# Narrow score blocks in a two-layer attention trunk: one float32 product, or three rounded ones

## The chip, the cores and the metric

The kernel runs on one core of one Trainium2 chip. The metric is the device time of one execution in microseconds (us). A core has five engines with queues of their own: PE (TensorE: it loads a stationary operand of up to 128 x 128, "PEld" in the profile, and streams the columns of a moving operand past it), DVE (VectorE), ACT (ScalarE), POOL (GpSimd) and SP, which issues most of the transfers. Each engine works through its queue in order, and waits on semaphores for the others. Products are written to PSUM, everything else lies in SBUF.

## The reference, cut to what matters

256 tokens of width 2048 go through two layers. Each layer normalises, projects with one wide matrix, runs 16 attention heads of width 128, multiplies by a gate and projects back. All is float32.

```
# layer 0: 10 heads A (one shared key and value head; every query keeps its 64 best keys)
#          6 heads B (dilated bands)
# layer 1: 8 heads C (stick-breaking), 8 heads D (softmax with forget gates)
logits = einsum('bqhd,bshd->bhqs', qb, k) * HEAD_DIM ** -0.5     # every kind of head, masked causally
```

The tokens are two blocks of 128. A causal head needs three blocks of scores of 128 x 128: the first queries with the first keys, and the second queries with both halves of the keys. The first of these three is the "first block" below (for the heads C, whose scores are kept the other way round, it is the second keys with the second queries).

## The kernel before, in words

**Precision.** A float32 product on PE appears as two records in the trace. To get near float32 from rounded operands (type float32r, one record), the kernel splits a float32 tile into a high part, which ACT rounds, and a low part, which DVE makes as the difference, and adds three products: high x high, high x low, low x high. All projections go this way: line 264 makes the high part of a half piece of weights, line 265 the low part, and lines 300, 301 and 303 are the three products, for two blocks of tokens, 512 columns wide at most.

**Order of work.** project() runs through the 36 column groups of the four weight matrices (ORDER0, four groups P, ORDER1, four groups Q). Weights arrive by SP's queue (line 241), and are split three halves ahead (AHEAD). The heads are Python generators, started when the projection of their group is done. tick() counts projection work; one tick is one step of six products of 512 columns, and at each tick the generators whose delay has run out emit their next piece. So the heads' pieces lie between projection products in PE's queue, at places fixed when the program is written, and in the queues of ACT and DVE likewise.

**A head's scores.** turn() (line 358) transposes the rows of queries and keys by four PE transposes into one PSUM tile of 512 columns. For the heads B, C and D qk_turned() then makes, from that tile, `hi` (ACT, line 367, the last 384 columns, rounded), `f` (ACT, line 368, the first 256 columns, copied as float32) and `lo` (DVE, line 369, 384 columns). Two ticks later the scores are made. In softmax_head() (heads A, B, D) line 401 is the first block, one float32 product from `f`; the other two blocks are one group of 256 columns by three(), lines 373, 374 and 375: high x high, high x low, low x high. stick_head() (heads C) does the same with line 682. heads_a() does two heads at once, with lines 576, 577 and 578 in the place of 367 to 369, and with the shared keys in `kA` (float32, line 507), `kAh` and `kAl`, made once by keys_a(). Afterwards DVE reads the scores (line 408, or 685), ACT takes the exponentials (line 410), PE turns them (line 358), and weigh_out() multiplies them with the values in float32 (lines 384 to 386).

The index scores of heads A (index()) make their parts from a turned tile of 512 columns whole, on lines 524 (ACT, high) and 525 (DVE, low). Lines 656 to 660 are the cumulative sums of the forget gates, float32 products of odd shapes: lines 656 to 658 have 128 stationary columns and 8 moving ones, 659 and 660 have 8 stationary ones and 256 or 128 moving ones.

Of the kernel before, what the change touches and what calls it, by code (L numbers as in the profile page):

```python
# [7 lines left out]
F32 = mybir.dt.float32  # L8
BF16 = mybir.dt.bfloat16
F32R = mybir.dt.float32r  # L10
AF = mybir.ActivationFunctionType
OP = mybir.AluOpType
PSUM = bass.MemoryType.PSUM

P = 128
# [144 lines left out]
def trunk(ctx, tc, x, xT, g1, w0, wo0, w1, wo1, bf, gf, consts, rope, out):  # L160
    nc = tc.nc
    cp = ctx.enter_context(tc.tile_pool(name="cp", bufs=1))
    wp = ctx.enter_context(tc.tile_pool(name="wp", bufs=3))
    hp = ctx.enter_context(tc.tile_pool(name="hp", bufs=2))
# [30 lines left out]
    rr = cp.tile([P, 2, NT], F32, name="rr")  # L195
    nr1 = cp.tile([P, NT], F32, name="nr1")
    vA = hp.tile([P, NT, P], F32, name="vA", tag="vt", bufs=1)
    kA = hp.tile([P, P], F32, name="kA", tag="kA", bufs=1)
    kAh = hp.tile([P, SEQ], F32R, name="kAh", tag="kAh", bufs=1)
    kAl = hp.tile([P, SEQ], F32R, name="kAl", tag="kAl", bufs=1)  # L200
    ikh = hp.tile([P, 2, SEQ], F32R, name="ikh", tag="ikh", bufs=1)
# [3 lines left out]
    nbA = score  # L205
# [68 lines left out]
    def start(g):  # L274
        n = next(g, None)
        if n is not None:
            side.append([g, n])
# [83 lines left out]
    def qk_turned(srcs):  # L361

        pt = turn(srcs)
        f = hp.tile([P, 256], F32, name="qkf", tag="qkf", bufs=1)
        hi = hp.tile([P, 384], F32R, name="qkh", tag="qkh", bufs=1)
        lo = hp.tile([P, 384], F32R, name="qkl", tag="qkl", bufs=1)
        nc.scalar.activation(hi, pt[:, P:512], AF.Copy)
        nc.scalar.activation(f, pt[:, 0:256], AF.Copy)
        nc.vector.tensor_tensor(lo, pt[:, P:512], hi.bitcast(F32), op=OP.subtract)
        return f, hi, lo  # L370

    def three(o, ah, al, bh, bl):
        nc.tensor.matmul(o, ah, bh, start=True, stop=False)
        nc.tensor.matmul(o, ah, bl, start=False, stop=False)  # L374
        nc.tensor.matmul(o, al, bh, start=False, stop=True)

    def qk_of(t):
        f, hi, lo = t
        return f[:, 0:P], f[:, P:256], hi[:, 256:384], lo[:, 256:384], hi[:, 0:256], lo[:, 0:256]

    def weigh_out(pT, vs, u, sc, kt):

# [13 lines left out]

    def softmax_head(qk, nb, vs, u, rs, kt):

        q0, k0, q1h, q1l, kh, kl = qk
        pS = pa.tile([P, 384], F32, name="s", tag="s", bufs=1)  # L400
        nc.tensor.matmul(pS[:, 0:P], q0, k0, start=True, stop=True)  # L401
        three(pS[:, P:384], q1h, q1l, kh, kl)
        sn = hp.tile([P, 384], F32, name="sn", tag="sn", bufs=2)
        nm = hp.tile([P, NT], F32, name="nm", tag="nm", bufs=2)
        pr = hp.tile([P, 384], F32, name="pr", tag="pr", bufs=2)
        l = hp.tile([P, NT], F32, name="l", tag="l", bufs=2)
        for th, s in BLK:
            nc.vector.tensor_tensor_reduce(sn[:, s], pS[:, s], nb[:, s], op0=OP.add, op1=OP.min, scale=1.0,  # L408
                                           scalar=3.0e38, accum_out=nm[:, th:th + 1])
            nc.scalar.activation(pr[:, s], sn[:, s], AF.Exp, scale=-1.0, bias=nm[:, th:th + 1],  # L410
                                 accum_out=l[:, th:th + 1])
        yield 3
        pt = turn([pr[:, 0:P], pr[:, P:SEQ], pr[:, SEQ:384]])
        pT = hp.tile([P, 384], F32, name="pT", tag="pT", bufs=2)
        nc.scalar.activation(pT, pt[:, 0:384], AF.Copy)  # L415
        sc = hp.tile([P, NT], F32, name="sc", tag="sc", bufs=2)
        nc.vector.reciprocal(sc, l)
        nc.vector.tensor_tensor(sc, sc, rs, op=OP.mult)
        yield 2
        yield from weigh_out([pT[:, i * P:(i + 1) * P] for i in range(3)], vs, u, sc, kt)  # L420
# [75 lines left out]
    def keys_a(ps):  # L496
        kr = hp.tile([P, 512], F32, name="kr", tag="qk")
        for th in range(NT):
            rotate(kr[:, th * P:(th + 1) * P], ps[th][:, 0:P], rt[:, th, P:2 * P], rt[:, th, 3 * P:4 * P], 1, P)
            o = 256 + th * P  # L500
            rotate(kr[:, o:o + DI], ps[th][:, 256:320], rt[:, th, 512:576], rt[:, th, 576:640], 1, DI)
            nc.gpsimd.tensor_copy(kr[:, o + DI:o + P], kr[:, o:o + DI])
            nc.scalar.activation(vA[:, th, :], ps[th][:, P:2 * P], AF.Copy, scale=r0[:, th:th + 1])
            nc.vector.tensor_scalar(iw[:, th, :], ps[th][:, 320:336], r0[:, th:th + 1], None, op0=OP.mult)
        yield 4
        pt = turn([kr[:, i * P:(i + 1) * P] for i in range(4)])
        nc.scalar.activation(kA, pt[:, 0:P], AF.Copy)
        nc.scalar.activation(kAh, pt[:, 0:256], AF.Copy)
        nc.vector.tensor_tensor(kAl, pt[:, 0:256], kAh.bitcast(F32), op=OP.subtract)
        for j in range(2):  # L510
            d = slice(j * DI, (j + 1) * DI)
            nc.scalar.activation(ikh[d, j], pt[d, 256:512], AF.Copy)
            nc.vector.tensor_tensor(ikl[d, j], pt[d, 256:512], ikh[d, j].bitcast(F32), op=OP.subtract)
# [47 lines left out]
    def heads_a(ps, h):  # L561
        qk = hp.tile([P, 512], F32, name="qk", tag="qk")
        u = hp.tile([P, 2, NT, P], F32, name="u2", tag="u2", bufs=1)
        for th in range(NT):
            rotate(qk[:, th * 256:(th + 1) * 256], ps[th][:, 0:256], rt[:, th, 0:P], rt[:, th, 256:384], 2, P)
            tg = hp.tile([P, 256], F32, name="tg", tag="tg")
            nc.scalar.activation(tg, ps[th][:, 256:512], AF.Tanh, scale=hr0[:, th:th + 1])
            nc.vector.scalar_tensor_tensor(u[:, :, th, :], tg.rearrange("p (a b) -> p a b", a=2), 1.0,
                                           ps[th][:, 256:512].rearrange("p (a b) -> p a b", a=2),
                                           op0=OP.add, op1=OP.mult)  # L570
        yield 4
        pt = turn([qk[:, 0:P], qk[:, P:256], qk[:, 256:384], qk[:, 384:512]])
        f = hp.tile([P, 256], F32, name="qqf", tag="qkf", bufs=1)
        hi = hp.tile([P, 256], F32R, name="qqh", tag="qkh", bufs=1)
        lo = hp.tile([P, 256], F32R, name="qql", tag="qkl", bufs=1)
        nc.scalar.activation(hi, pt[:, 256:512], AF.Copy)
        nc.scalar.activation(f, pt[:, 0:256], AF.Copy)
        nc.vector.tensor_tensor(lo, pt[:, 256:512], hi.bitcast(F32), op=OP.subtract)
        yield 2
        js = [slice(j * P, (j + 1) * P) for j in range(2)]  # L580
        hs = [softmax_head((f[:, js[j]], kA, hi[:, js[j]], lo[:, js[j]], kAh, kAl), nbA, [vA[:, 0], vA[:, 1]],
                           u[:, j].rearrange("p a b -> p (a b)"), hr0, YPOS[f"A{h + j}"]) for j in range(2)]
        start(delay(hs[1], 2))
        yield from hs[0]

    def delay(g, n):
        yield n
        yield from g
# [88 lines left out]

    def stick_head(qk, v, u, kt):

        k1, q1, k0h, k0l, qh, ql = qk  # L680
        pZ = pa.tile([P, 384], F32, name="s", tag="s", bufs=1)
        nc.tensor.matmul(pZ[:, 0:P], k1, q1, start=True, stop=True)
        three(pZ[:, P:384], k0h, k0l, qh, ql)
        z = hp.tile([P, 384], F32, name="z", tag="sn")
        nc.vector.tensor_tensor(z, pZ, smask, op=OP.add)
        sp = hp.tile([P, 384], F32, name="sp", tag="pr")
        nc.scalar.activation(sp, z, AF.Abs)
        nc.scalar.activation(sp, sp, AF.Exp, scale=-1.0)
        nc.scalar.activation(sp, sp, AF.Ln, bias=1.0)
        nc.vector.scalar_tensor_tensor(sp, z, 0.0, sp, op0=OP.max, op1=OP.add)  # L690
        hi, lo = sph[:, P:512], spl[:, P:512]
        nc.scalar.activation(hi, sp, AF.Copy)
        nc.vector.tensor_tensor(lo, sp, hi.bitcast(F32), op=OP.subtract)
        yield 5
        pW = pa.tile([P, 384], F32, name="s", tag="s", bufs=1)
        nc.tensor.matmul(pW, tris[0], hi, start=True, stop=False)
        nc.tensor.matmul(pW, tris[0], lo, start=False, stop=False)
        nc.tensor.matmul(pW[:, 0:256], tris[1], sph[:, 0:256], start=False, stop=False)
        nc.tensor.matmul(pW[:, 0:256], tris[1], spl[:, 0:256], start=False, stop=True)
        w = hp.tile([P, 384], F32, name="wT", tag="pT")  # L700
        nc.vector.tensor_tensor(w, pW, z, op=OP.add)
        nc.scalar.activation(w, w, AF.Exp)
        yield 3
        yield from weigh_out([w[:, 256:384], w[:, P:256], w[:, 0:P]], [v[:, 0], v[:, 1]], u, r1, kt)
# [158 lines left out]
```

## Time and profile before

| what | value |
|---|---|
| median of the three runs | 934.88 us (934.54 to 936.18) |
| the profiled execution | 935.72 us |
| its span, first to last instruction | 933.9 us |
| mean granted TensorE clock | 0.996 |
| busy: PE, PEld | 921.2 us, 772.4 us |
| busy: DVE, ACT, POOL | 592.0 us, 474.8 us, 43.8 us |
| moved from and to HBM | 165.89 MB read, 2.11 MB written, 180 GB/s |

Times are from the hardware profiler, of one execution. PE is TensorE's product stream and PEld its weight loads, which run beside the products; ends of products are modelled, so the distance from one product to the next, as the chain of waits has it, says more than a record's own length. "<-" in a row reads "made from"; "x2" merges two records. In the chain of waits each row is a piece of the chain that ended last: its start, its length and what it was. A bracket in a timeline holds the time for which the engine stood idle before the instruction, and what ended it. Tile names are the program's: `qkh`, `qkl` and `qkf` are `hi`, `lo` and `f` of a head, `qqh`, `qql` and `qqf` those of a pair of heads A, `s` is the scores, `pj` a projection, `tp` a turned tile.

### The profile page before, as it was taken

The numbers are of one execution on the slowest core, as the hardware profiler recorded it, in microseconds if no ns is written. First come the engines' busy times: TensorE is split into PE (matmuls) and PEld (weight loads), VectorE is DVE, ScalarE is ACT, GpSimd is POOL, SyncE is SP. The second block draws the span as 40 slices with busy tenths as digits, with TensorE's granted clock in tenths as the row PEclk, the third lists the DMA queues.
The fourth block names the chain that finished last, engine by engine and source line by source line (L and its number), as shares of the span: only waits on it lengthen the run. The fifth ranks groups of instructions, "written<-read, shape, count | busy, mean of one in ns | idle before, by whom it ended". The sixth has DMA issues, their size and how long they took to land.

```text
span 933.9 us, 12009 instructions
## 1 busy us (share of the span) xinstructions
PE 921.2 (99%) x4537; PEld 772.4 (83%) x4537; DVE 592.0 (63%) x982; ACT 474.8 (51%) x805; POOL 43.8 (5%) x63
## 2 busy tenths in 40 slices
PE   9999999999999999999999999999999999999996
PEld 6978888888888888888898888888888888888876
DVE  7657777756556556555566666666766666665553
ACT  7654454544545545544456555555555444554441
POOL 0002100000000000000000000000000000001110
PEclk9999999999999999999999999999999999999998
DMA  9854445544455445555356444444655555455542
GB/s 346 342 180 175 144 172 181 175 169 139 150 180 180 163 156 178 180 184 189 126 171 245 159 157 165 160 175 180 231 186 186 172 172 174 175 180 180 182 179 91
DMA packets 27754, 168.77 MB, mean 181 GB/s; under 512 B 3224, under 2 KB 4784, under 8 KB 9520
## 3 DMA queue, kind: packets, MB, share of 16 engines
q1 hardware_dynamic: 26208, 165.24, 50.0%
q0 software_dynamic: 768, 2.12, 0.8%
q8 instruction: 35, 0.57, 0.2%
q10 hardware_dynamic: 720, 0.66, 0.2%
q14 instruction: 23, 0.19, 0.1%
HBM read 165.89 MB, written 2.11 MB: 180 GB/s over the span
## 4 chain that ended last, share of the span: by engine, by line
PE 92%; DMA 3%; issue 2%; ACT 1%; DVE 1%; SPq 0%; DVEq 0%; POOLq 0%; POOL 0%; ACTq 0%
PE pj L300 28%; PE pj L303 27%; PE pj L301 27%; PE tp L358 3%; DMA xs<-in_x_dram 1%; PE o L386 1%; PE o L385 1%; PE o L384 1%; DMA xst<-in_xT_dram 1%; DMA raw<-in_w_in_dram 1%; ACT sq L424 1%; DMA w0yh<-in_w_in_dram 1%; PE s L401 1%; ACT whi L264 0%; PE s L374 0%
## 5 line engine op out<-in xcount | busy, mean ns | idle before, releaser
L265 DVE TENSOR_TENSOR wlo<-raw,whi 128x1024 fp32r<-128x1024 f32 (+3 forms) x300 | 355.3, 1199 | 193.0 <-ACT whi L264 192.1
L300 PE MATMUL pj<-whi,xh 128*128 128x512 f32 (+3 forms) x992 | 387.3, 392 | 0.9 <-ACT whi L264 0.7
L301 PE MATMUL pj<-whi,xl 128*128 128x512 f32 (+3 forms) x992 | 377.0, 382 | 0.0
L264 ACT ACTIVATE whi<-raw 128x1024 fp32r<-128x1024 f32 (+3 forms) x300 | 302.0, 1025 | 133.3 <-PE pj L301 130.0
L303 PE MATMUL pj<-wlo,xh 128*128 128x512 f32 (+3 forms) x992 | 298.1, 382 | 0.1
L303 PEld LDWEIGHTS pj<-wlo,xh 128*128 128x128 f32 x992 | 183.5, 188 | 37.5 <-DVE wlo L265 0.9
L300 PEld LDWEIGHTS pj<-whi,xh 128*128 128x128 f32 x992 | 187.0, 188 | 33.1 <-ACT whi L264 2.5
L301 PEld LDWEIGHTS pj<-whi,xl 128*128 128x128 f32 x992 | 187.1, 189 | 30.4
L300 PE MATMUL pj<-whi,yh 128*128 128x512 f32 (+1 forms) x248 | 96.2, 388 | 0.0
L301 PE MATMUL pj<-whi,yl 128*128 128x512 f32 (+1 forms) x248 | 94.9, 383 | 0.0
L303 PE MATMUL pj<-wlo,yh 128*128 128x512 f32 (+1 forms) x248 | 76.7, 383 | 0.0
L303 PEld LDWEIGHTS pj<-wlo,yh 128*128 128x128 f32 x248 | 46.6, 188 | 9.2
L300 PEld LDWEIGHTS pj<-whi,yh 128*128 128x128 f32 x248 | 46.7, 188 | 8.6
L301 PEld LDWEIGHTS pj<-whi,yl 128*128 128x128 f32 x248 | 46.7, 188 | 8.5
L410 ACT ACTIVATE pr<-sn,nm 128x128 f32<-128x128 f32 (+1 forms) x48 | 21.5, 448 | 47.8 <-DVE nm L408 47.8
L394 ACT ACTIVATE yh<-tp 128x256 fp32r<-128x256 f32 x32 | 12.3, 385 | 57.5 <-PE tp L358 57.4
L395 DVE TENSOR_TENSOR yl<-tp,yh 128x256 fp32r<-128x256 f32 x32 | 13.6, 425 | 25.9 <-ACT yh L394 25.0
L424 ACT ACTIVATE sq<-xs 128x512 f32<-128x512 f32 x23 | 14.3, 623 | 30.3 <-DVE xs L594 27.7
L637 DVE RECIPROCAL e<-e 128x256 f32<-128x256 f32 x16 | 28.1, 1754 | 0.5
L353 POOL TENSOR_TENSOR qk<-rot,rot 128x256 f32<-128x256 f32 x22 | 16.0, 738 | 239.8 <-DVE rot L352 239.8
L415 ACT ACTIVATE pT<-tp 128x384 f32<-128x384 f32 x24 | 11.7, 485 | 20.9 <-PE tp L358 20.9
L623 ACT ACTIVATE qk<-pj,rr 128x128 f32<-128x128 f32 x32 | 10.0, 364 | 21.3 <-PE pj L303 21.3
(203 smaller groups left out, 703.8 us busy)
## 6 DMA issues: line engine op xcount, KB each, us to landing
raw<-in_w_in_dram SPq DMA_DIRECT2D x108, 1024.0 KB, 4.8
raw<-in_w_out_dram SPq DMA_DIRECT2D x32, 1024.0 KB, 4.8
raw<-in_w_in_dram SPq DMA_DIRECT2D x4, 672.0 KB, 9.4
raw<-in_w_in_dram SPq DMA_DIRECT2D x4, 528.0 KB, 3.5
w0yl<-in_w_in_dram SPq DMA_DIRECT2D x4, 512.0 KB, 8.2
xs<-in_x_dram SPq DMA_DIRECT2D x2, 1024.0 KB, 11.3
raw<-in_w_in_dram SPq DMA_DIRECT2D x4, 512.0 KB, 3.9
xst<-in_xT_dram SPq DMA_DIRECT2D x5, 256.0 KB, 7.0
```

What stands on the lines that cost most here:

```text
L264: nc.scalar.activation(hi, rw, AF.Copy)
L265: nc.vector.tensor_tensor(lo, rw, hi.bitcast(F32), op=OP.subtract)
L300: nc.tensor.matmul(o, a, wh, start=(kt == 0), stop=False)
L301: nc.tensor.matmul(o, b, wh, start=False, stop=False)
L303: nc.tensor.matmul(o, a, wl, start=False, stop=(kt == KT - 1))
L353: nc.gpsimd.tensor_tensor(dst, t1[:, 0:n], t2[:, 0:n], op=OP.add)
L358: nc.tensor.transpose(pt[:, i * P:(i + 1) * P], s, ident)
L394: nc.scalar.activation(yh[:, kt, :], pt[:, 0:SEQ], AF.Copy)
L395: nc.vector.tensor_tensor(yl[:, kt, :], pt[:, 0:SEQ], yh[:, kt, :].bitcast(F32), op=OP.subtract)
L410: nc.scalar.activation(pr[:, s], sn[:, s], AF.Exp, scale=-1.0, bias=nm[:, th:th + 1], accum_out=l[:, th:th + 1])
L424: nc.scalar.activation(j, xs[:, th, c * 512:(c + 1) * 512], AF.Square, accum_out=ss[:, i, th, c:c + 1])
L637: nc.vector.reciprocal(e, e)
```

## The change

qk_turned() and heads_a() no longer make the float32 copy `f`. `hi` and `lo` cover all 512 columns of the turned tile. A new function scores() makes a head's first block as three rounded products of 128 columns in the order of three(), ahead of the group of 256 columns, which is as it was; softmax_head() and stick_head() call it. The float32 copy `kA` of the first keys goes, and the heads A use the first 128 columns of `kAh` and `kAl`. Nothing else changes.

```diff
@@ -195,7 +195,6 @@
     rr = cp.tile([P, 2, NT], F32, name="rr")
     nr1 = cp.tile([P, NT], F32, name="nr1")
     vA = hp.tile([P, NT, P], F32, name="vA", tag="vt", bufs=1)
-    kA = hp.tile([P, P], F32, name="kA", tag="kA", bufs=1)
     kAh = hp.tile([P, SEQ], F32R, name="kAh", tag="kAh", bufs=1)
     kAl = hp.tile([P, SEQ], F32R, name="kAl", tag="kAl", bufs=1)
     ikh = hp.tile([P, 2, SEQ], F32R, name="ikh", tag="ikh", bufs=1)
@@ -361,13 +360,11 @@
     def qk_turned(srcs):
 
         pt = turn(srcs)
-        f = hp.tile([P, 256], F32, name="qkf", tag="qkf", bufs=1)
-        hi = hp.tile([P, 384], F32R, name="qkh", tag="qkh", bufs=1)
-        lo = hp.tile([P, 384], F32R, name="qkl", tag="qkl", bufs=1)
-        nc.scalar.activation(hi, pt[:, P:512], AF.Copy)
-        nc.scalar.activation(f, pt[:, 0:256], AF.Copy)
-        nc.vector.tensor_tensor(lo, pt[:, P:512], hi.bitcast(F32), op=OP.subtract)
-        return f, hi, lo
+        hi = hp.tile([P, 512], F32R, name="qkh", tag="qkh", bufs=1)
+        lo = hp.tile([P, 512], F32R, name="qkl", tag="qkl", bufs=1)
+        nc.scalar.activation(hi, pt, AF.Copy)
+        nc.vector.tensor_tensor(lo, pt, hi.bitcast(F32), op=OP.subtract)
+        return hi, lo
 
     def three(o, ah, al, bh, bl):
         nc.tensor.matmul(o, ah, bh, start=True, stop=False)
@@ -375,8 +372,15 @@
         nc.tensor.matmul(o, al, bh, start=False, stop=True)
 
     def qk_of(t):
-        f, hi, lo = t
-        return f[:, 0:P], f[:, P:256], hi[:, 256:384], lo[:, 256:384], hi[:, 0:256], lo[:, 0:256]
+
+        hi, lo = t
+        return hi[:, 0:P], lo[:, 0:P], hi[:, 384:512], lo[:, 384:512], hi[:, P:384], lo[:, P:384]
+
+    def scores(o, qk):
+
+        ah, al, bh, bl, mh, ml = qk
+        three(o[:, 0:P], ah, al, mh[:, 0:P], ml[:, 0:P])
+        three(o[:, P:384], bh, bl, mh, ml)
 
     def weigh_out(pT, vs, u, sc, kt):
 
@@ -396,10 +400,8 @@
 
     def softmax_head(qk, nb, vs, u, rs, kt):
 
-        q0, k0, q1h, q1l, kh, kl = qk
         pS = pa.tile([P, 384], F32, name="s", tag="s", bufs=1)
-        nc.tensor.matmul(pS[:, 0:P], q0, k0, start=True, stop=True)
-        three(pS[:, P:384], q1h, q1l, kh, kl)
+        scores(pS, qk)
         sn = hp.tile([P, 384], F32, name="sn", tag="sn", bufs=2)
         nm = hp.tile([P, NT], F32, name="nm", tag="nm", bufs=2)
         pr = hp.tile([P, 384], F32, name="pr", tag="pr", bufs=2)
@@ -504,7 +506,6 @@
             nc.vector.tensor_scalar(iw[:, th, :], ps[th][:, 320:336], r0[:, th:th + 1], None, op0=OP.mult)
         yield 4
         pt = turn([kr[:, i * P:(i + 1) * P] for i in range(4)])
-        nc.scalar.activation(kA, pt[:, 0:P], AF.Copy)
         nc.scalar.activation(kAh, pt[:, 0:256], AF.Copy)
         nc.vector.tensor_tensor(kAl, pt[:, 0:256], kAh.bitcast(F32), op=OP.subtract)
         for j in range(2):
@@ -570,15 +571,14 @@
                                            op0=OP.add, op1=OP.mult)
         yield 4
         pt = turn([qk[:, 0:P], qk[:, P:256], qk[:, 256:384], qk[:, 384:512]])
-        f = hp.tile([P, 256], F32, name="qqf", tag="qkf", bufs=1)
-        hi = hp.tile([P, 256], F32R, name="qqh", tag="qkh", bufs=1)
-        lo = hp.tile([P, 256], F32R, name="qql", tag="qkl", bufs=1)
-        nc.scalar.activation(hi, pt[:, 256:512], AF.Copy)
-        nc.scalar.activation(f, pt[:, 0:256], AF.Copy)
-        nc.vector.tensor_tensor(lo, pt[:, 256:512], hi.bitcast(F32), op=OP.subtract)
+        hi = hp.tile([P, 512], F32R, name="qqh", tag="qkh", bufs=1)
+        lo = hp.tile([P, 512], F32R, name="qql", tag="qkl", bufs=1)
+        nc.scalar.activation(hi, pt, AF.Copy)
+        nc.vector.tensor_tensor(lo, pt, hi.bitcast(F32), op=OP.subtract)
         yield 2
         js = [slice(j * P, (j + 1) * P) for j in range(2)]
-        hs = [softmax_head((f[:, js[j]], kA, hi[:, js[j]], lo[:, js[j]], kAh, kAl), nbA, [vA[:, 0], vA[:, 1]],
+        j1 = [slice(256 + j * P, 256 + (j + 1) * P) for j in range(2)]
+        hs = [softmax_head((hi[:, js[j]], lo[:, js[j]], hi[:, j1[j]], lo[:, j1[j]], kAh, kAl), nbA, [vA[:, 0], vA[:, 1]],
                            u[:, j].rearrange("p a b -> p (a b)"), hr0, YPOS[f"A{h + j}"]) for j in range(2)]
         start(delay(hs[1], 2))
         yield from hs[0]
@@ -677,10 +677,8 @@
 
     def stick_head(qk, v, u, kt):
 
-        k1, q1, k0h, k0l, qh, ql = qk
         pZ = pa.tile([P, 384], F32, name="s", tag="s", bufs=1)
-        nc.tensor.matmul(pZ[:, 0:P], k1, q1, start=True, stop=True)
-        three(pZ[:, P:384], k0h, k0l, qh, ql)
+        scores(pZ, qk)
         z = hp.tile([P, 384], F32, name="z", tag="sn")
         nc.vector.tensor_tensor(z, pZ, smask, op=OP.add)
         sp = hp.tile([P, 384], F32, name="sp", tag="pr")
```

## Rows read from the trace of the kernel before

**Rows 1.** The page of the kernel before: span, busiest engine, chain that ended last.
```profile
span 933.9 us, 12009 instructions
...
PE 921.2 (99%) x4537; PEld 772.4 (83%) x4537; DVE 592.0 (63%) x982; ACT 474.8 (51%) x805; POOL 43.8 (5%) x63
...
PE pj L300 28%; PE pj L303 27%; PE pj L301 27%; PE tp L358 3%; DMA xs<-in_x_dram 1%; PE o L386 1%; PE o L385 1%; PE o L384 1%; DMA xst<-in_xT_dram 1%; DMA raw<-in_w_in_dram 1%; ACT sq L424 1%; DMA w0yh<-in_w_in_dram 1%; PE s L401 1%; ACT whi L264 0%; PE s L374 0%
```

**Rows 2.** Chain of waits on PE, 840 to 842.2 us: start us, us, what.
```profile
841.04 0.22 PE s L401 x2
841.26 0.12 PE s L373
...
841.62 0.23 PE pj L300
```

**Rows 3.** Costliest groups by line and shape: busy us, mean ns, then idle before.
```profile
L369 DVE TENSOR_TENSOR qkl<-tp,qkh 128x384 fp32r<-128x384 f32 x22 | 12.1, 551 | 2.5 <-ACT qkf L368 2.5
...
L367 ACT ACTIVATE qkh<-tp 128x384 fp32r<-128x384 f32 x22 | 10.8, 492 | 15.7 <-PE tp L358 15.7
...
L368 ACT ACTIVATE qkf<-tp 128x256 f32<-128x256 f32 x22 | 8.4, 381 | 0.0
...
L401 PE MATMUL s<-qkf 128*128 128x128 f32 x28 | 5.3, 272 | 0.0
...
L525 DVE TENSOR_TENSOR il<-tp,ih 128x512 fp32r<-128x512 f32 x4 | 2.7, 684 | 1.1 <-ACT ih L524 1.1
...
L524 ACT ACTIVATE ih<-tp 128x512 fp32r<-128x512 f32 x4 | 2.4, 599 | 4.8 <-PE tp L358 4.8
```

**Rows 4.** Chain of waits, 469.9 to 473 us and 486 to 490 us.
```profile
469.85 0.33 PE tp L358 x3
...
488.31 0.22 PE s L657 x2
...
489.28 0.22 PE s L660 x2
```

**Rows 5.** Timeline of head C0 at 473 us: start us, us, instruction, [idle].
```profile
472.80 0.31 PEld L682 LDWEIGHTS s<-qkf 128*128 128x128 f32 x2
472.84 0.55 DVE L369 TENSOR_TENSOR qkl<-tp,qkh 128x384 fp32r<-128x384 f32 x1
...
473.44 0.19 PEld L374 LDWEIGHTS s<-qkl,qkh 128*128 128x128 f32 x1 [0.22 <-DVE qkl L369]
...
473.55 0.19 PEld L375 LDWEIGHTS s<-qkh,qkl 128*128 128x128 f32 x1
```

**Rows 6.** Timeline, heads C2 (524 us) and D7 (840 us): start, us, instruction.
```profile
524.53 0.55 DVE L369 TENSOR_TENSOR qkl<-tp,qkh 128x384 fp32r<-128x384 f32 x1
...
525.16 0.38 PE L682 MATMUL s<-qkf 128*128 128x128 f32 x2
...
840.27 0.55 DVE L369 TENSOR_TENSOR qkl<-tp,qkh 128x384 fp32r<-128x384 f32 x1
...
840.88 0.38 PE L401 MATMUL s<-qkf 128*128 128x128 f32 x2
```

**Rows 7.** Timeline of a pair of heads A at 231 us.
```profile
231.14 0.42 DVE L578 TENSOR_TENSOR qql<-tp,qqh 128x256 fp32r<-128x256 f32 x1
...
232.73 0.38 PE L401 MATMUL s<-kA,qqf 128*128 128x128 f32 x2
```

**Rows 8.** Chain of waits, 40 to 60 us, and timeline of PE there.
```profile
44.51 0.30 DVE qkl L369
...
44.92 0.38 PE L401 MATMUL s<-qkf 128*128 128x128 f32 x2
...
51.70 0.33 PE L358 MATMUL tp<-cons,pr 128*128 128x128 f32 x1 [1.96 <-ACT pr L410]
```

**Rows 9.** Waits of PE's weight loads over the span: us, times, longest.
```profile
PEld s L374 <- DVE qkl L369: 0.2, 1, 0.2
```

**Rows 10.** Busy us by stretch: PE, PEld, DVE, ACT, POOL, then granted clock.
```profile
50.00:55.00 5.00, 3.13 (x11) 2.65 (x12) 3.27 (x9) 2.86 (x9) 0.00 (x0) 0.70 0.60 208
```

## The prediction

> **What bounds the kernel now.** I read the page first. PE is busy for 921.2 of 933.9 us, and the chain that ended last runs for 82% of the span through the projection products of lines 300, 301 and 303 [rows 1]. DVE and ACT are busy for 592.0 and 474.8 us. So a nanosecond added to PE's stream is a nanosecond of the end, nearly everywhere, and work taken from ACT is worth nothing unless PE waits for it. A busy PE is not PE at its peak, so I read next what one product really takes: in the chain of waits a projection product of 512 columns takes 0.23 us, a rounded product of 256 columns 0.12, and the float32 product of a head's first block 0.22, in two records of 0.11 each [rows 2]. The reader is to see there that the first block, of 128 columns, costs as much as a projection product of 512.
>
> Third, the groups by line give the durations on ACT and DVE, and the number of records: 28 on line 401 for the 14 heads of kinds B and D, so two to a product [rows 3]. Last, the timelines around the scores, to see what PE's next weight load would wait for [rows 5 to 8]. Over the whole span a score waits for its low part once, for 0.2 us [rows 9]. How near the other heads are to such a wait is the second question here.
>
> **What the change does, part by part.**
>
> *Products.* There are 32 heads (6 B, 10 A, 8 C, 8 D). Each loses one float32 product, two records, 0.22 us in the chain [rows 2], and gets three rounded products of 128 columns. The kernel before has no rounded product as narrow as that, so its cost has to be bounded. From below: if only the moving columns counted, the line through 256 columns at 0.12 and 512 at 0.23 [rows 2] gives 0.12 - 128 x 0.11/256 = 0.065 us. From above: each as long as the whole float32 product, 0.22. Between them stand the rows of short products. Line 657 multiplies 128 loaded columns with 8 moving ones, and its two records take 0.22, as much as the 128 moving columns of a score; line 660 has 8 loaded columns and 128 moving ones and takes 0.22 as well [rows 4]. So a weight load of 128 columns takes 0.11 by itself, however little moves behind it, and a float32 record of 128 moving columns takes 0.11 too. The transposes, one record of 128 by 128, also take 0.11 each [rows 4]. That rounded operands don't load faster is seen at head C0: after a wait that left nothing to hide behind, the load of line 375 starts 0.11 us behind that of line 374, both rounded [rows 5]. That row is the nearest to the new product, so I take 0.11: three cost 0.33, 0.11 more than now. For 32 heads that is 3.5 us; with 31 of them (B0 stands below) 3.4 us. The ends are -0.8 us (32 x (3 x 0.065 - 0.22)) and +14.1 us (32 x 0.44).
>
> One rule speaks for a smaller term: the Trainium skill, page "TensorE: Matmul & The Clock Gate", section "Back-to-back issue gap", gives about 81 ns per load and product of 128 columns in a sustained stream. By it three would take 0.24 us and the term would be an estimated 0.7 us instead of 3.5; the trace disagrees, at 0.11 us each in the transposes [rows 4].
>
> *ACT.* A head of kind B, C or D now rounds 384 columns in 492 ns and copies 256 in 381; it will round 512 in one instruction, for which line 524 gives 599 [rows 3]. That is 274 ns less, 22 times: 6.0 us of ACT time. The A pairs and the copy of line 507 shrink likewise. It is worth nothing: in all the heads whose low part is late (next part), DVE starts it right behind other work of its own, long after ACT is done.
>
> *DVE, and the wait that moves.* The low part grows from 384 to 512 columns, 551 to 684 ns by line 525 [rows 3], so it lands 0.13 us later. And it is wanted sooner: today PE runs the two float32 records and line 373 before the first product that reads the low part; in the new order it is the second of the three narrow products. Its load can start when the first product starts to stream, which is where the first float32 record starts now. For head C2 that is 525.16 us, and the low part would be there at 524.53 + 0.684 = 525.21, and 0.05 later for PE (the lag at C0: 472.84 + 0.55 against the load at 473.44 [rows 5]): a wait of 0.10 us. For D7 it is 840.27 + 0.684 + 0.05 = 841.00 against 840.88, a wait of 0.12 [rows 6]. All 14 heads from C2 to D7 look like one of these two: 14 x 0.11 = 1.6 us. At C0 the wait exists already: the low part would be seen at 472.84 + 0.684 + 0.05 = 473.57, then come four loads of 0.11 (the second narrow product's, the third's, line 373's, then line 374's at 473.90) where line 374's is at 473.44 now [rows 5]; 0.46 later, of which 0.11 is counted above, so 0.35 us. The A pairs have room: 0.42 becomes 0.684 from 231.14 on, and PE comes at 232.73 [rows 7]. So have B1 to B5 and C1, whose low parts end well before PE comes.
>
> What queues behind the longer DVE instruction is the next low part of the weights, which is used several microseconds later; the bound for that delay is nothing as long as PE doesn't wait for line 265.
>
> *B0.* PE would lose 0.11 + 0.32 us there (44.51 + 0.684 + 0.05 against 44.92), but it stands idle for 1.96 us at 51.70, and the chain of that stretch runs through DVE, with this very low part in it [rows 8]. So PE's loss is covered, and DVE's 0.13 us counts. The granted clock falls to 0.70 in the 5 us around that idle time [rows 10]; if the idle time moves or shrinks, that is worth up to 0.3 x 5 = 1.5 us either way, which I keep for the range.
>
> No transfer and no issue on SP or POOL moves. The buffers that go or grow are on-chip and their sum stays within a kilobyte; I give that nothing.
>
> **Sum:** 3.4 + 1.6 + 0.35 + 0.13 = 5.5 us, 0.6%. The profiled execution took 935.72 us with a span of 933.9 [rows 1]; the median of the runs shown is 934.88, 0.84 below it. On the median the forecast is 940.4 us.
>
> **The rivals.**
>
> *The waits don't come.* If DVE gets to the low part 0.13 us sooner (ACT is freer ahead of it), only the products and B0 count: 3.5 us, 938.4. Against it: at the 14 heads DVE's queue is full in front of it. Chance 0.15.
>
> *Narrow rounded products run no faster than float32.* Nothing in the trace shows rounded operands under 256 columns, and the kernel might lose their speed there. At 0.22 each the products cost 14.1 us, and the waits vanish beneath them: 949. For it there is only the absence of such rows; against it, that 256 columns cost hardly more than half of 512 [rows 2]. Chance 0.10.
>
> *The moving columns set the pace, not the loads (not slower).* If PE can hide the loads of three products in a row, each takes 0.065: -0.8 us, plus the waits' 2.0 and B0's 0.13 give 1.3 us, 936.2, no change that can be measured. It decides where a load of 128 columns takes under 0.075 us, since then three cost no more than the 0.22 of now. Against it: line 657 and the loads at C0, both 0.11. The Trainium skill ("FP8 and Floating Point Precision", "TensorE Precision Notes") counts four passes for a float32 product; against three that would save a quarter of 0.22, an estimated 1.8 us, were it the passes that are paid. Chance 0.07.
>
> *Anything else*, such as the clock around 52 us: 0.03.
>
> **How the numbers follow.** The forecast has a chance of 0.65, its own range 939.0 to 941.9. A difference under 0.2% (1.9 us) can't be told from none. Slower is the sum of the forecast and the first two rivals, 0.90; same is 0.08, the third rival and a third of the rest; faster 0.02. The range goes down to 937.5 (the first rival, less 0.9 for half of the clock's stake) and up to 943.5 (the forecast with the waits doubled, 1.6, and the clock's 1.5): it leaves out the other two rivals and the rest, 0.20.
>
> **What would show it.** In the chain of waits the three narrow products take 0.33 us where the float32 pair took 0.22; if they show 0.2 or 0.66, the second or third rival holds. Among the waits of PE's weight loads, the low part of the score appears some 14 times with about 0.1 us each and once with 0.6 at C0. ACT's busy time falls by 6 us or more and DVE's rises by about 4 without either changing the end. A gain in time, or narrow loads closer than 0.11 us with no wait, would prove me wrong.

## The result, and the profile after

The changed kernel took 940.44 us (median of 4 runs, 939.13 to 942.2), the kernel before 934.71 beside it (4 runs). The ratio is 1.0061, 95% interval 1.0043 to 1.0079: slower by 5.7 us. The profiled execution took 942.2 us.

The page of the changed kernel, lines that answer to [rows 1]: span, busy time of the engines, the chain by line, and ACT's high part, which is one instruction of 512 columns now.

```profile
span 940.4 us, 12008 instructions
...
PE 928.0 (99%) x4569; PEld 777.8 (83%) x4569; DVE 596.1 (63%) x982; ACT 471.7 (50%) x777; POOL 43.8 (5%) x63
...
PE pj L299 29%; PE pj L300 29%; PE pj L302 29%; PE tp L357 3%; PE s L371 1%; PE s L372 1%; PE s L370 1%; PE o L390 1%; PE o L389 1%; PE o L388 1%; PE tp L606 0%; DMA w0yh<-in_w_in_dram 0%; PE s L535 0%; PE s L534 0%; PE s L536 0%
...
L365 ACT ACTIVATE qkh<-tp 128x512 fp32r<-128x512 f32 x22 | 13.2, 600 | 15.7 <-PE tp L357 15.7
```

PE is busy for 6.8 us more and the span is 6.5 us longer. ACT has lost 3.1 us net and DVE has gained 4.1, without showing in the chain; the scores take more of it than before (1% on each of lines 370 to 372, where [rows 1] has 1% on line 401 and less on line 374).

Chain of waits on PE, in the stretch of a pair of heads A, the place of [rows 7]. Start us, us, what:

```profile
234.10 0.06 PE s L370
234.16 0.11 PE s L371
234.27 0.11 PE s L372
234.38 0.17 PE s L370
234.55 0.12 PE s L371
234.67 0.12 PE s L372
234.79 0.23 PE pj L299
```

These are the six products of one head. Together they take 0.69 us where the five records of [rows 2] took 0.22 + 3 x 0.12 = 0.58. The first of them seems cheap, 0.06: its load lay beneath the 512 columns before it, and only its own 128 columns are seen. So the three narrow rows add up to 0.28, not to the 0.33 that the prediction named as its sign; the other 0.05 stands in the row behind them. The loads of the second, the third and the first wide product come one per 0.11, and the last of these is paid by the wide product, which takes 0.17 rather than 0.12. So one reads such a group as a whole: the three narrow products and the first wide one make 0.45 us, where the float32 pair and line 373 made 0.22 + 0.12 = 0.34.

Head D7 in the chain, the place of [rows 2]:

```profile
847.35 0.06 PE s L370
847.41 0.24 PE s L371
847.65 0.11 PE s L372
```

And in the timeline of DVE and of PE's loads, the place of [rows 6]:

```profile
846.58 0.69 DVE L366 TENSOR_TENSOR qkl<-tp,qkh 128x512 fp32r<-128x512 f32 x1
...
846.97 0.19 PEld L370 LDWEIGHTS s<-qkh 128*128 128x128 f32 x1
...
847.32 0.19 PEld L371 LDWEIGHTS s<-qkl,qkh 128*128 128x128 f32 x1 [0.17 <-DVE qkl L366]
...
847.43 0.19 PEld L372 LDWEIGHTS s<-qkh,qkl 128*128 128x128 f32 x1
```

Here the second product takes 0.24. Its load starts 0.35 us behind the first one's instead of 0.23 (the distance at heads that don't wait, seen in the rows of the low part in two, below), since the low part ends at 846.58 + 0.69 = 847.27 and is seen 0.05 later. The wait of 0.12 us is the one that was forecast. The loads at head C0, against [rows 5]:

```profile
475.28 0.19 PEld L370 LDWEIGHTS s<-qkh 128*128 128x128 f32 x1
476.05 0.19 PEld L371 LDWEIGHTS s<-qkl,qkh 128*128 128x128 f32 x1 [0.58 <-DVE qkl L366]
476.16 0.19 PEld L372 LDWEIGHTS s<-qkh,qkl 128*128 128x128 f32 x1
```

0.77 us from the first load to the second, of which the row has 0.58 as idle time, the wait of about 0.6 that was forecast for C0. The waits of PE's loads over the span, the place of [rows 9]:

```profile
PEld s L371 <- DVE qkl L366: 1.8, 8, 0.6
```

They wait for the low part 8 times by this view (C0 and D1 to D7; at C2 to C7 and D0 they wait too, by the distance of their loads, but so briefly that the view doesn't count them) where it was once, for 0.2 us [rows 9].

How the loss grows is seen from where the heads' scores start. Rows of the changed kernel that answer to [rows 5 to 7]:

```profile
233.94 0.22 PE L370 MATMUL s<-kAh,qqh 128*128 128x128 f32 x1
...
528.23 0.22 PE L370 MATMUL s<-qkh 128*128 128x128 f32 x1
...
847.19 0.22 PE L370 MATMUL s<-qkh 128*128 128x128 f32 x1
```

The second A pair is late by 233.94 - 232.73 = 1.21 us, C0 by 475.28 - 472.80 = 2.48, C2 by 528.23 - 525.16 = 3.07, D7 by 847.19 - 840.88 = 6.31. Ten heads without a wait lie between the first two: 0.127 us each. C0 and C1 make 0.59. Then 13 heads with a wait make 3.24: 0.249 each.

### The profile page after: what moved, and what is told of

It reads as the page before. It is cut to its first block, busy times and chain, and to the rows that moved or that the text cites. A ratio compares the mean times of both kernels' runs of the same rounds, so it can differ in the third digit from the quotient of the medians.

```text
span 940.4 us, 12008 instructions
## 1 busy us (share of the span) xinstructions
PE 928.0 (99%) x4569; PEld 777.8 (83%) x4569; DVE 596.1 (63%) x982; ACT 471.7 (50%) x777; POOL 43.8 (5%) x63
## 4 chain that ended last, share of the span: by engine, by line
PE 96%; issue 1%; DVE 1%; ACT 1%; DMA 0%; POOLq 0%; DVEq 0%; POOL 0%; SPq 0%; ACTq 0%
PE pj L299 29%; PE pj L300 29%; PE pj L302 29%; PE tp L357 3%; PE s L371 1%; PE s L372 1%; PE s L370 1%; PE o L390 1%; PE o L389 1%; PE o L388 1%; PE tp L606 0%; DMA w0yh<-in_w_in_dram 0%; PE s L535 0%; PE s L534 0%; PE s L536 0%
## 5 line engine op out<-in xcount | busy, mean ns | idle before, releaser
L365 ACT ACTIVATE qkh<-tp 128x512 fp32r<-128x512 f32 x22 | 13.2, 600 | 15.7 <-PE tp L357 15.7
```

What stands on the lines that cost most here:

```text
L365: nc.scalar.activation(hi, pt, AF.Copy)
```

## The experiments

Two measures are given: the time, beside runs of the kernel before that were timed with it, and, from the traces, the stretch from the start of head B1's first score product to that of head D7's. That stretch leaves out the end, and the first 130 us, in which executions of one kernel differ by a few microseconds (more on that below). It is 706.68 us in the kernel before.

```
run                       us      beside  ratio (95% interval)       B1 to D7, us more
changed kernel            940.44  934.71  1.0061 (1.0043 to 1.0079)   5.74
changed kernel again      939.83  934.06  1.0061 (1.0047 to 1.0074)   5.77
high products first       939.43  934.06  1.0051 (1.0038 to 1.0063)   4.31
low part in two           939.70  934.06  1.0056 (1.0042 to 1.0070)   3.90
wide parts, float32       935.02  934.06  1.0007 (0.9998 to 1.0016)   0.15
more loads                950.78  935.68  1.0160 (1.0142 to 1.0177)  15.97
more columns              941.49  935.68  1.0063 (1.0046 to 1.0080)   6.29
before, late turn         933.46  935.06  0.9983 (0.9974 to 0.9992)   0.01
changed, late turn        939.18  935.06  1.0045 (1.0032 to 1.0057)   5.84
high first, late turn     937.74  935.06  1.0029 (1.0016 to 1.0041)   4.20
low in two, late turn     937.37  934.18  1.0027 (1.0016 to 1.0038)   3.89
before, later still       932.09  934.18  0.9973 (0.9962 to 0.9983)   0.02
```

### The changed kernel again

> The changed kernel once more, timed beside the variants. Both theories: 1.006 of the kernel before, some 940.4 us; in the trace 32 heads whose three narrow products take 0.33 us in the chain, and some 15 waits of 0.1 us (0.55 at C0) on the low part.

1.0061 as before. The stretch from B1 to D7 repeats to 0.03 us (5.74 and 5.77), while B1 itself starts at 131.64 us here and at 134.77 in the first profile. So steps of a few tens of nanoseconds per head can be read from two traces, though the times of single executions scatter by 2 to 3 us.

### Loads or columns: the two rivals on the products

```diff
-        three(o[:, 0:P], ah, al, mh[:, 0:P], ml[:, 0:P])
+        n = o[:, 0:P]
+        nc.tensor.matmul(n, ah, mh[:, 0:P], start=True, stop=False)
+        nc.tensor.matmul(n, ah, ml[:, 0:P], start=False, stop=False)
+        for c in range(0, P, 32):
+            nc.tensor.matmul(o[:, c:c + 32], al, mh[:, c:c + 32], start=False, stop=(c == 96))
```

> The changed kernel, with the third narrow product (low x high) cut into four of 32 columns each: the columns stay 128, the weight loads grow by three per head. If loads set the pace: 4 x 0.11 in the place of 0.11, 0.33 us per head, 32 x 0.33 = 10.5 us more, about 951 us, and the chain shows 0.11 per piece. If the moving columns set the pace: nothing, 940.4 us.

950.78 us. In B1 to D7 it is 15.97 - 5.77 = 10.2 us more than the changed kernel, over 30 heads 0.34 each, or 0.11 per added load. The weight loads of this kernel at a pair of heads A (start, us, x4 merged):

```profile
233.82 0.19 PEld L384 LDWEIGHTS s<-kAl,qqh 128*128 128x128 f32 x1
233.93 0.53 PEld L386 LDWEIGHTS s<-kAh,qql 128*128 128x128 f32 x4
234.37 0.19 PEld L370 LDWEIGHTS s<-kAh,qqh 128*128 128x128 f32 x1
```

Four loads in 234.37 - 233.93 = 0.44 us, with no more than 32 columns behind each. The columns per head are the same as in the changed kernel. "The moving columns set the pace" is out for narrow products. All four pieces have the same stationary operand, and each loads it anew; on the page of the changed kernel above, too, there are as many loads as products, 4569.

These runs add a load and a product together, so they leave open whether 0.11 us is the price of any load, however small. Two rows of the kernel before answer that, at the cumulative sums of the forget gates, with 128 and with 8 stationary columns:

```profile
488.36 0.30 PEld L658 LDWEIGHTS s<-logf,cons 128*128 128x128 f32 x2
...
488.68 0.10 PEld L659 LDWEIGHTS s<-cons,logf 128*8 128x8 f32 x2
```

Two loads of 128 columns take 0.30 us together, two loads of 8 columns are over in 0.10. So it is the 128 columns of a load that cost 0.11.

```diff
-        three(o[:, 0:P], ah, al, mh[:, 0:P], ml[:, 0:P])
+        three(o[:, 0:256], ah, al, mh, ml)
```

> The changed kernel, with 256 moving columns in each of the three narrow products in the place of 128 (the second half is overwritten by the wide group that follows, so the scores are the same): twice the columns, the same loads. If loads set the pace: 0.12 instead of 0.11 per product, 96 x 0.01 = 1.0 us more, about 941.4 us. If the moving columns set the pace: 96 x 0.055 = 5.3 us more, about 945.7 us. If rounded products under 256 columns lost their speed and cost more per column for that, it would be faster than the changed kernel.

941.49 us; 6.29 - 5.77 = 0.52 us more from B1 to D7, in 90 products of twice the columns: 6 ns each. (At heads B1 to B5, which don't wait for the low part, it is 9 ns each, 0.154 us more per head than in the kernel before in the place of 0.127; at the heads that wait, part of it goes into the wait.) The chain, six products of 256 columns:

```profile
235.64 0.12 PE s L370
235.75 0.12 PE s L371
...
236.35 0.23 PE pj L299
```

0.12 each, 0.71 for the six instead of 0.69. So 128 columns more cost less than a tenth of what a load costs. The rival that narrow rounded products run like float32, at 0.22, is out with it, as it was by the 0.11 of the views above. A narrow product that paid twice per column would hide behind the load, at 0.11; but the first of the six, whose load lies beneath the product before it, takes 0.06 with 128 columns and 0.12 with 256, which speaks against that too.

The Trainium skill gives both sides of this. "TensorE: Matmul & The Clock Gate", section "LDWEIGHTS (loading the stationary operand)", puts a load at its columns over 1.2 GHz, an estimated 107 ns for 128, and the traces agree (0.11 in each of the views above). Section "Back-to-back issue gap" of that page of the Trainium skill puts a sustained load and product of 128 columns at about 81 ns; no run here shows the loads of two such score products less than 0.11 us apart.

### What waits for the low part

```diff
-        three(o[:, 0:P], ah, al, mh[:, 0:P], ml[:, 0:P])
-        three(o[:, P:384], bh, bl, mh, ml)
+        n, w = o[:, 0:P], o[:, P:384]
+        nc.tensor.matmul(n, ah, mh[:, 0:P], start=True, stop=False)
+        nc.tensor.matmul(w, bh, mh, start=False, stop=False)
+        nc.tensor.matmul(n, ah, ml[:, 0:P], start=False, stop=False)
+        nc.tensor.matmul(n, al, mh[:, 0:P], start=False, stop=False)
+        nc.tensor.matmul(w, bh, ml, start=False, stop=False)
+        nc.tensor.matmul(w, bl, mh, start=False, stop=True)
```

> The same six rounded products per head in another order: both high x high products first, so that the low part is wanted 0.11 us later. My theory (products 3.4 us, waits 2.0 us): the waits of the 14 heads C2 to D7 vanish or fall to 0.02 us, C0 keeps all but 0.11, B0 gains nothing: 1.6 us less than the changed kernel, 4.1 us over the kernel before, about 938.8 us. Rival (the loss is the products alone, the waits are hidden elsewhere): no change, 940.4 us. Rival (the loss is DVE's and ACT's): no change either.

From B1 to D7 it is 5.77 - 4.31 = 1.46 us less than the changed kernel (13 heads with a wait and C0 lie in that stretch; at 0.10 and 0.11 each, 13 x 0.10 + 0.11 = 1.4 of the forecast 1.6 fall to them). The view of the waits for the low part shrinks to one, C0's, 0.11 shorter or so as forecast (at D1 to D7 some 0.01 us are left by the distance of the loads):

```profile
PEld s L385 <- DVE qkl L366: 0.5, 1, 0.5
```

The time was 939.43 against 939.83, only 0.4 less, and the intervals overlap: the first 130 us hide it. The late turn (below) takes that away.

```diff
-            nc.vector.tensor_tensor(lo, pt, hi.bitcast(F32), op=OP.subtract)
+            for c in (slice(0, 256), slice(256, 512)):
+                nc.vector.tensor_tensor(lo[:, c], pt[:, c], hi[:, c].bitcast(F32), op=OP.subtract)
```

> The changed kernel with the low part made by two DVE instructions of 256 columns, the first of which carries what the narrow products read. It lands at 0.42 us instead of 0.68, DVE works some 0.08 us longer per head. My theory: at D7 it is there 0.14 us before PE wants it, so the 14 waits vanish, C0's falls by 0.26: 1.8 us less than the changed kernel, about 938.6 us, although DVE has more to do. Rival (DVE's busy time is what costs): 27 x 0.08 = 2.2 us more, 942.6 us. Rival (waits hidden elsewhere): 940.4 us.

1.87 us less than the changed kernel from B1 to D7 (5.77 - 3.90), with more work for DVE. The time, 939.70, again scatters too much to say so. At D7 the two halves take 0.74 us in all. PE's second load comes 0.23 us behind the first, as where nothing waits, and the third 0.11 behind the second:

```profile
841.95 0.74 DVE L367 TENSOR_TENSOR qkl<-tp,qkh 128x256 fp32r<-128x256 f32 x2
...
842.33 0.19 PEld L371 LDWEIGHTS s<-qkh 128*128 128x128 f32 x1
...
842.56 0.19 PEld L372 LDWEIGHTS s<-qkl,qkh 128*128 128x128 f32 x1
...
842.67 0.19 PEld L373 LDWEIGHTS s<-qkh,qkl 128*128 128x128 f32 x1
```

The kernel before with wide parts, of which the first 128 (A pairs: 256) columns are made and not read:

```diff
-        f = hp.tile([P, 256], F32, name="qkf", tag="qkf", bufs=1)
-        hi = hp.tile([P, 384], F32R, name="qkh", tag="qkh", bufs=1)
-        lo = hp.tile([P, 384], F32R, name="qkl", tag="qkl", bufs=1)
-        nc.scalar.activation(hi, pt[:, P:512], AF.Copy)
+        f = hp.tile([P, 256], F32, name="qkf", tag="tg")
+        hi = hp.tile([P, 512], F32R, name="qkh", tag="qkh", bufs=1)
+        lo = hp.tile([P, 512], F32R, name="qkl", tag="qkl", bufs=1)
+        nc.scalar.activation(hi, pt, AF.Copy)
         nc.scalar.activation(f, pt[:, 0:256], AF.Copy)
-        nc.vector.tensor_tensor(lo, pt[:, P:512], hi.bitcast(F32), op=OP.subtract)
+        nc.vector.tensor_tensor(lo, pt, hi.bitcast(F32), op=OP.subtract)
...
```

> The kernel before, with its float32 product and float32 copy, but the high and low parts over all 512 columns as in the changed kernel (the copy lies in a buffer of the gates, to make room; the new first columns of the parts are not read). ACT works 0.11 us longer per head than before, DVE 0.13. My theory: the products are as before and line 374 wants the low part 0.23 us later than the changed kernel does, after it has landed, so only C0 (0.13) and B0 (0.13) lose: 935.0 us, no difference that can be measured. Rival (the longer work on DVE is paid wherever it stands): 27 x 0.13 = 3.5 us, 938.2 us.

935.02 us, ratio 1.0007, no difference that can be told. From B1 to D7 0.15 us more, nearly all of it at C0, where the wait grows as forecast:

```profile
PEld s L374 <- DVE qkl L369: 0.4, 1, 0.4
```

So neither the 4 us more of DVE nor more work for ACT cost anything that can be told. What costs is the low part's end together with the place at which PE asks for it.

### The stretch around 52 us

The scatter of the times comes from the place where the prediction put B0's cover [rows 8, 10]. In the second profile of the changed kernel PE stood idle there for 0.31 us instead of 1.96, and the granted clock stayed at 1.00:

```profile
50.65 0.33 PE L357 MATMUL tp<-cons,pr 128*128 128x128 f32 x1 [0.31 <-ACT pr L412]
```

Busy time by stretch there, columns as in [rows 10]:

```profile
50.00:55.00 5.00, 4.53 (x25) 3.49 (x24) 2.62 (x9) 3.16 (x9) 0.00 (x0) 1.00 0.61 210
```

How long PE idles depends there on when DVE and ACT finish with the first loads, which varies between executions. To take that out, B0's exponentials are turned three ticks later:

```diff
-        yield 3
+        yield 6 if kt == 0 else 3
         pt = turn([pr[:, 0:P], pr[:, P:SEQ], pr[:, SEQ:384]])
```

> The kernel before, with head B0's exponentials turned six ticks after its scores in the place of three, so that PE works on projections of I0 where it stood idle for 1.96 us at 51.70. The weights of several halves lie ready there. My theory: the idle time goes and with it the fall of the granted clock to 0.70: some 2.0 + 1.5 us less, about 931 us, and runs that differ less from each other. Rival (the stretch is bound by the arrival of the first transfers): PE idles later instead, 934 us.

933.46 us, 1.6 less where 3.5 were expected, ratio 0.9983 (0.9974 to 0.9992), and all executions within 0.9 us. Both stories hold in part: the idle time at 51.70 and the fall of the clock are gone, but a new wait of 1.17 us has come at 58.84:

```profile
58.84 0.49 PE L384 MATMUL o<-v,pT 128*128 128x128 f32 x2 [1.17 <-ACT pT L415]
```

Busy time by stretch, with the granted clock at 1.00 in both:

```profile
50.00:55.00 5.00, 5.00 (x28) 4.16 (x26) 3.31 (x7) 2.37 (x7) 0.00 (x0) 1.00 0.56 193
55.00:60.00 5.00, 3.83 (x20) 2.99 (x19) 3.45 (x7) 4.20 (x6) 0.00 (x0) 1.00 0.11 28
```

The changed kernel, and the order with the high products first, with the same late turn:

> The changed kernel with the same later turn of B0. With the idle time at 52 us gone from both, the change is to cost its products and waits alone: by the traces from head B1 to the end 6.0 us, with B0's own 0.1 to 0.4 in addition since its cover is gone: 6.1 to 6.4 us over the kernel before with the late turn, about 937.3 us. Rival (part of the cost came from that stretch): under 5 us.

> Both high x high products first (as e1_high_first) and the late turn of B0. My theory: without the scatter of the stretch at 52 us the 1.6 us that the trace shows from B1 on are seen in the time too: 1.6 to 1.9 us under the changed kernel with the late turn. Rival (they are lost again later): under 0.8 us.

> The changed kernel with the low part in two DVE instructions (as e5_split_low) and the late turn of B0. My theory (PE waits for the last column of the low part, not for DVE's work as such): 1.9 us under the changed kernel with the late turn, as the traces without the late turn show from B1 on, although DVE has more to do. Rival (DVE's work costs): slower than the changed kernel with the late turn.

With the late turn the changed kernel takes 939.18 us, 5.7 more than the kernel before with it. 6.1 to 6.4 was expected, and the spans of the two profiled executions are 6.5 apart (938.1 and 931.6); from B1 to D7 it is 5.83 more (5.84 - 0.01). Why the medians are closer isn't shown; one difference ahead of B1 is the new wait at the weighted values of B0, 0.9 us where it was 1.2. High products first takes 937.74, 1.4 less than the changed kernel with the late turn, where 1.6 to 1.9 was expected; its slowest execution (938.12) is faster than the fastest of the other (938.70). The low part in two takes 937.37 (beside other runs of the kernel before; by the ratios, 1.0045 and 1.0027, 1.7 less, where 1.9 was expected). So the waits are real time, as the traces said.

The wait at 58.84 goes too, if B0's weighted values come two ticks later still (kernel before, with the late turn):

```diff
-        yield 2
+        yield 4 if kt == 0 else 2
         yield from weigh_out([pT[:, i * P:(i + 1) * P] for i in range(3)], vs, u, sc, kt)
```

> The kernel before with the late turn of B0, and its weighted values two ticks later still (four in the place of two), since with the late turn PE idled for 1.17 us at 58.84 for ACT's copy of the turned exponentials. My theory: that idle time goes too: about 1.1 us under the kernel with the late turn alone, 932.3 us. Rival (ACT's copy waits for something that only moves along): the same as with the late turn alone, 933.4 us.

932.09 us, ratio 0.9973 (0.9962 to 0.9983): 2.1 us (0.27%) faster than the kernel before, and 8 us faster than the changed one. Neither 51.70 nor 58.84 is among the waits of PE's products that are left. The first two of these lie in the first 6 us, the third at 905:

```profile
PE s L772 <- DVE mhalf L773: 1.2, 1, 1.2
PE pj L300 <- ACT whi L264: 0.6, 1, 0.6
PE pj L303 <- DVE xl L265: 0.5, 1, 0.5
```

## Why the prediction was right, step by step

The time was forecast as 940.4 us and came to 940.44. That the two agree to a tenth is luck, since single executions differ by 3 us; the terms are what can be compared.

**The products (3.4 us forecast).** Right in kind: the price is the load, 0.11 us, as lines 657 and 375 had shown in the kernel before, and both rivals on it are out (more loads, more columns). The size was a little low. The chain has 0.11 us more per head, but ten heads without a wait lose 0.127 each, so 31 lose 3.9 us. The traces show where the other 0.016 us lie, though not why: at each of these heads the first projection product behind the six is 0.11 us late and the sixth one 0.13, and no more is added after that. The prediction counted the group alone, and not the products behind it.

**The waits (1.6 us at 14 heads, 0.35 at C0).** Right. C2 and D7 wait 0.10 and 0.12 us by their loads, 13 heads from C2 on lose 0.249 - 0.127 = 0.12 each, so 14 lose 1.7; C0 and C1 together lost 0.59, of which 0.59 - 2 x 0.127 = 0.34 is C0's wait. The rival that the waits don't come has fallen: an order that asks later and a low part that lands earlier each win them back, by two ways that share nothing but the wait.

**B0 (0.13 us).** The figure can't be tested. In neither profile of the changed kernel does PE wait for B0's low part, so the 0.32 us that were to be lost there and covered were not lost at all; in the profile with the late turn it does wait, and the second load comes 0.33 us later than at heads that don't. What happens ahead of B1 differs between executions: B1's scores start 0.57 us later in one profile of the changed kernel and 2.56 us earlier in the other. The prediction kept 1.5 us either way for that stretch; it was worth twice that, since the idle time itself varies and not only the clock after it. The kernel before varies there too, so little of it is left between medians. (Half of that stake is 0.75 us, not the 0.9 that the lower end of the range takes off for it; nothing else hangs on that.)

**ACT and DVE (nothing).** Right: wide parts alone are not to be told from the kernel before. But ACT's busy time fell by 3.1 us and not by 6 or more. The durations of the lines are as forecast (line 365 takes 13.2 us where lines 367 and 368 took 10.8 + 8.4 [rows 3]); what failed is taking them for busy time. Added up, ACT's rows have 7.2 us less. But successive instructions of ACT overlap in the rows, and the page counts that time once. The kernel before, ACT's timeline at D7:

```profile
838.30 0.49 ACT L367 ACTIVATE qkh<-tp 128x384 fp32r<-128x384 f32 x1 [0.51 <-PE tp L358]
...
838.69 0.38 ACT L368 ACTIVATE qkf<-tp 128x256 f32<-128x256 f32 x1
...
838.96 1.06 ACT L264 ACTIVATE whi<-raw 128x1024 fp32r<-128x1024 f32 x1
```

Line 368 starts 0.10 us before 367 ends, and the next instruction 0.11 before 368 ends. So of the 0.38 us of line 368 only 0.17 were busy time of its own.

**Sum.** 3.9 + 1.7 + 0.34 = 6.0 us, against 6.5 - 0.57 = 5.9 from B1 to the end of the profiled span, and 5.7 between the medians.

## What to carry to other kernels

When PE is always busy, count weight loads, not multiplications, and count a load for every product, even where the stationary operand is the one before. As long as a product had no more than 256 rounded columns, it cost about what its load of 128 columns took here, 0.11 to 0.12 us. So three cheap products were dearer than one float32 product of two loads, and widening them was nearly free. When a split into parts is widened, look at both ends of the wait: how much later the last part lands, and how much earlier the new order asks for it; issuing all that needs the high parts first gave 1.4 us back. And where executions scatter, read a stretch between two marks in the traces: 0.03 us repeated, where times moved by 3 us.

## What was not expected of the hardware

The granted clock did not follow the length of the idle time alone. PE idled for 1.96 us in the kernel before and 5 us of the stretch show 0.70 [rows 10]; in the changed kernel 1.53 us of idle time brought 0.90 and then 0.76:

```profile
52.19 0.33 PE L357 MATMUL tp<-cons,pr 128*128 128x128 f32 x1 [1.53 <-ACT pr L412]
```

Its busy time by stretch:

```profile
50.00:55.00 5.00, 3.31 (x15) 2.29 (x15) 3.14 (x8) 2.71 (x8) 0.00 (x0) 0.90 0.53 169
55.00:60.00 5.00, 5.00 (x21) 4.15 (x20) 3.42 (x8) 2.76 (x4) 0.00 (x0) 0.76 0.10 41
```

But the kernel with more columns idled for 1.62 us at the same place and stayed at 1.00, and so did the kernel before with the late turn after its 1.17:

```profile
51.73 0.33 PE L357 MATMUL tp<-cons,pr 128*128 128x128 f32 x1 [1.62 <-ACT pr L412]
```

Its busy time by stretch:

```profile
50.00:55.00 5.00, 3.22 (x17) 2.55 (x17) 3.28 (x9) 2.58 (x7) 0.00 (x0) 1.00 0.61 202
55.00:60.00 5.00, 5.00 (x26) 4.24 (x25) 3.45 (x6) 3.83 (x5) 0.00 (x0) 1.00 0.16 28
```

Means like 0.70 and 0.76 mix the two levels, 1.2 and 2.4 GHz. What decides between them for idle times of 1.5 to 2 us can't be told from these runs.
